# One head a step instead of two, and column loads two steps ahead, in a hybrid SSD and linear-attention layer

## The chip, the cores and the metric

The kernel runs on one core of a Trainium2 chip. The metric is the device time of one execution in microseconds, as a median over runs. The core has a matrix engine (TensorE, PE in the profile; its weight loads are shown apart as PEld), three engines for elementwise work (VectorE or DVE, ScalarE or ACT, GpSimd or POOL), and SyncE (SP), which in this kernel only issues transfers. Transfers are also issued from ScalarE's queue.

## The reference

One layer of a decoder runs over 16 meta tokens and 2048 real tokens of width 1024, in float32. A single input projection of the normed input feeds two branches: a Mamba-2 branch (SSD, 16 heads in 4 groups) and gated linear attention (GLA, 4 heads with key width 128 and value width 256). Each branch is projected, gated and merged, and the layer ends with an output projection and two RMS norms. Cut to what this change touches:

```python
u = rmsnorm(hres, norm_w)
proj = jnp.einsum('bld,dn->bln', u, w_in)
z, xbc, dt_raw, q, k, v, g_gla, a_lr, merge_g = split_cols(proj, IN_WIDTHS)
...
gate_logit = jnp.einsum('blr,rk->blk', a_lr, gla_gate_w2) + gla_gate_b
log_a = (jax.nn.log_sigmoid(gate_logit.astype(jnp.float32)) / GLA_GATE_TEMP)
log_a = log_a.reshape(b, l, GLA_HEADS, GLA_HEAD_K)
...
gc = jnp.cumsum(to_chunks(log_a).astype(jnp.float32), axis=3)
...
g_last = gi[:, :, -1]
k_dec = ki * jnp.exp(g_last[:, :, None, :] - gi)
s_new = jnp.exp(g_last)[..., None] * s + jnp.einsum('bhsk,bhsv->bhkv', k_dec, vi)
```

So the decay of a GLA head is a projection of rank 16 followed by a log-sigmoid and a cumulative sum along time; it is small beside the projections of `u`.

## The kernel before

**Two parts.** The first part, up to about 1500 us, does all that is sequential: the norm, the feature projections, the convolution, both scans. The second part does the merge gates, the two branch projections and the output projection as Strassen-like products of half-size blocks. Every product of the projections is made of three matmuls of values split into a high and a low float32r part (`accum`, L187 to L191).

**Blocks and steps.** The first part goes through four blocks of 512 tokens (block 0 also has the 16 meta tokens, and so processes its columns in two segments of 264). A block has eight units: four SSD groups (`ssd_proj`) and four GLA heads (`gla_proj`), of six steps each. All the work that isn't the projection itself is written as Python generators (the scans, the decays, the load of the next block, partial sums for the second part). After every step of a projection, `step()` advances each running generator to its next `yield`, so a `yield` decides between which projections an instruction stands.

**Order.** Within `manual_schedule`, TensorE and SyncE take their instructions in program order. The orders of VectorE, ScalarE and GpSimd are made by a planner that simulates the program when it is built; at run time each engine works strictly in its order.

**Banks and slots.** PSUM pool `pj` has three banks (`bufs=3`); a projection of block 0 takes two at once, of the later blocks one, and a token projection (`proj_tok`) of z or v holds two over its two steps. A bank or slot is taken again when all that read it are through. Weights lie in four slots (`whl`, `load_w`, L165), raw weights and operands of the partial sums in four (`wr`).

**The decays.** `gates(o)` begins with SSD group 1 of each block. Its first step transposes the low-rank activations. Then, for each pair of heads, one step makes both heads' projections (L485), empties each bank twice (L487 on VectorE, L488 on ScalarE) and applies Exp and Ln to the pair (L490, L491); two further steps do the subtraction and the cumulative sums (L494, L496). The first `gla_scan`, which reads the result, begins after the first GLA unit.

**The next block's columns.** `fetch_u(b + 1)` begins with the first GLA unit of a block. Its generator `load_u` first loads the next block's rows and makes the reciprocal norms (five steps). Then it loads the transposed input in eight columns of 128 x 512 (`fetch`, L308 to L311, into tag `acc`, four slots), and in each of eight steps issues the next column's load, scales the present one (L253, VectorE), copies its high part (L257, ScalarE), stores it to memory from ScalarE's queue (L259), and subtracts for the low part (L262, VectorE). The loads are issued by SP, whose queue also carries the weights (L169, L173), the saving of split weights (L185) and the loads and stores of partial sums (L76, L88). If a slot isn't free, SP waits at the load, and all behind it with it.

**Where the scans wait.** In `gla_scan`, four chunks follow each other: TensorE multiplies with the state (L880), VectorE updates the state (L883), and the next chunk's L880 needs it. L794 is a small VectorE copy in the scans of block 0 that a TensorE transpose (L796) needs.

Of the kernel before, what the change touches and what calls it, by code (L numbers as in the profile page):

```python
# [16 lines left out]
KT = 8  # L17
META = 16
BLK = 512
# [21 lines left out]
def trunk_kernel(ctx: ExitStack, tc: tile.TileContext, xm, xmt, w_feat, w_tok, w_zm, w_br, w_o,  # L41
# [7 lines left out]
    def mk(pool, shape, dt, tag, **kw):  # L49
        cnt[0] += 1  # L50
        return pool.tile(shape, dt, tag=tag, name=f"{tag}_{cnt[0]}", **kw)
# [83 lines left out]
    def bank(pool, tag):  # L135
        return mk(pool, [P, 512], F32, tag)
# [111 lines left out]
    def u_pair(tt):  # L248
        pair = mk(upool, [P, 2, KT * (META + BLK)], F32R, "u")[:, :, :KT * tt]
        return [pair[:, i].rearrange("p (k t) -> p k t", k=KT) for i in range(2)]  # L250

    def scale_u(kt, xk, rbc):
        nc.vector.scalar_tensor_tensor(xk, xk, norm_w[:, kt:kt + 1], rbc, op0=ALU.mult, op1=ALU.mult)  # L253

    def to_u(b, kt, xk, uh, ul):
        m0 = 0 if b else META
        nc.scalar.activation(uh[:, kt, :m0 + BLK], xk, AF.Copy)  # L257
        if b:
            nc.scalar.dma_start(u_left[b][kt], xk[:, m0:])  # L259
        else:  # L260
            u_stores.append((u_left[b][kt], xk[:, m0:]))
        nc.vector.tensor_tensor(ul[:, kt, :m0 + BLK], xk, uh[:, kt, :m0 + BLK].bitcast(F32), op=ALU.subtract)  # L262
# [41 lines left out]
    def load_u(b):  # L304
        row0 = META + b * BLK
        uh, ul = u_pair(BLK)

        def fetch(src):  # L308
            xt = mk(wk, [P, META + BLK], F32, "acc", bufs=4)[:, :BLK]
            nc.sync.dma_start(xt, src)  # L310
            return xt  # L311

        def fetch_rows(c):
            r0 = row0 + c * P
            return [fetch(xm[r0:r0 + P, i * BLK:(i + 1) * BLK]) for i in range(2)]

        def rows_rstd(xts, n):
            ss = mk(sm, [P, 1], F32, "ss")
            s2 = mk(sm, [P, 2], F32, "ss2")
            for i, xt in enumerate(xts):  # L320
                nc.scalar.activation(xt, xt, AF.Square, accum_out=s2[:, i:i + 1])
            nc.vector.tensor_tensor(ss, s2[:, 0:1], s2[:, 1:2], op=ALU.add)
            r = mk(sm, [P, 1], F32, "rs1")
            nc.vector.tensor_scalar(r[:n], ss[:n], 1.0 / D, EPS, op0=ALU.mult, op1=ALU.add)
            nc.gpsimd.tensor_tensor(r[:n], r[:n], mhalf[:n, 0:1], op=ALU.pow)
            return r

        rs = []
        rows = fetch_rows(0)
        yield  # L330
        for c in range(NCH):
            got, rows = rows, fetch_rows(c + 1) if c + 1 < NCH else None
            rs.append(rows_rstd(got, P))
            yield
        rb = bank(pt, "pt")
        for c in range(NCH):
            nc.tensor.matmul(rb[:, c * P:(c + 1) * P], rs[c].to_broadcast([P, P]), ident, start=True, stop=True)
        rbc = mk(wk, [P, 3 + META + BLK], F32, "cin")[:, :BLK]
        nc.scalar.activation(rbc, rb, AF.Copy)
        cols = [fetch(xmt[:, 0, row0:row0 + BLK])]  # L340
        yield
        for kt in range(KT):
            if kt + 1 < KT:
                cols.append(fetch(xmt[:, kt + 1, row0:row0 + BLK]))
            xk = cols[kt]
            scale_u(kt, xk, rbc)
            to_u(b, kt, xk, uh, ul)
            yield
        return uh, ul
# [3 lines left out]
    def fetch_u(b):  # L353
        next_u[b] = yield from load_u(b)
# [110 lines left out]
    def gates(o):  # L465
        m0, tt, chunks, g_all = o.m0, o.tt, o.chunks, o.g_all
        ast = mk(wk, [P, META + BLK], F32R, "act", bufs=NACT)[:48, :tt]
        for a, n in ([(0, META), (m0, BLK)] if m0 else [(0, BLK)]):
            ps = bank(pt, "pt")
            for i, (ca, cn) in enumerate(chunks):  # L470
                if a <= ca < a + n:
                    nc.tensor.transpose(ps[:48, ca - a:ca - a + cn], o.alr[:cn, i], ident[:cn, :cn])
            nc.scalar.activation(ast[:, a:a + n], ps[:48, :n], AF.Copy)
            nc.vector.tensor_tensor(ast[:32, a:a + n], ps[:32, :n], ast[:32, a:a + n].bitcast(F32),
                                    op=ALU.subtract)
            nc.scalar.activation(ast[:16, a:a + n], ps[:16, :n], AF.Copy)
        yield
        for h2 in range(0, GH, 2):
            gmt = mk(wk, [P, 2, META + BLK], F32, "tok4", bufs=NT4)
            for h in (h2, h2 + 1):  # L480
                gm = gmt[:, h % 2, :tt]
                gb = gate_b[:, h:h + 1]
                for i, (a, n) in enumerate(o.segs_all):
                    ps = bank(*((pt, "pt") if i else (pj, "pj")))
                    nc.tensor.matmul(ps[:, :n], w2[:, h * P:(h + 1) * P], ast[:, a:a + n],  # L485
                                     start=True, stop=True)
                    nc.vector.tensor_scalar(gm[:, a:a + n], ps[:, :n], gb, 0.0, op0=ALU.add, op1=ALU.min)  # L487
                    nc.scalar.activation(g_all[:, h, a:a + n], ps[:, :n], AF.Abs, bias=gb)  # L488
            ga = g_all[:, h2:h2 + 2, :tt]
            nc.scalar.activation(ga, ga, AF.Exp, scale=-1.0)  # L490
            nc.scalar.activation(ga, ga, AF.Ln, bias=1.0)  # L491
            yield
            for h in (h2, h2 + 1):
                nc.vector.tensor_tensor(gmt[:, h % 2, :tt], gmt[:, h % 2, :tt], g_all[:, h, :tt], op=ALU.subtract)  # L494
                for a, n in chunks:
                    nc.vector.tensor_tensor_scan(g_all[:, h, a:a + n], ones[:, :n], gmt[:, h % 2, a:a + n], 0.0,  # L496
                                                 op0=ALU.mult, op1=ALU.add)
                yield
# [424 lines left out]
    with tc.manual_schedule(engines={mybir.EngineType.PE, mybir.EngineType.SP}):  # L923
        for b in range(nblk):
            o = new_block(b, next_u[b])
            for i in range(SG + GH):
                if (b, i) in beside:
                    begin(beside_unit(beside[b, i]))
                if i == 1:
                    begin(gates(o))  # L930
                if i == SG and b + 1 < nblk:
                    begin(fetch_u(b + 1))
                for _ in ssd_proj(o, i) if i < SG else gla_proj(o, i - SG):
                    step()
            save(0)
        while running or begun:
            step()
# [326 lines left out]
```

## Time and profile before

| | |
|---|---|
| runs | 2295.11, 2302.26, 2309.61 us (median 2302.26) |
| profiled execution | 2299.73 us, of which the span from the first to the last instruction is 2297.9 us |
| TensorE busy | 2229.1 us (97%) |
| VectorE busy | 1604.1 us (70%) |
| ScalarE busy | 1119.9 us (49%) |
| GpSimd busy | 709.8 us (31%) |
| transfers | 507.49 MB, mean 221 GB/s |

All times within the run are in microseconds from the start of the span. Matmuls overlap in the pipeline and their ends are modelled, so a busy TensorE isn't one at its peak. The granted clock of TensorE (PEclk) is 1.00 at full speed. A wait is put down to the instruction that ended it; where VectorE is in the way, the cause can stand further ahead in VectorE's order. L numbers are lines of the kernel before.

### The profile page before, as it was taken

To read this page: it belongs to the slowest core of one execution; us is meant where nothing else is said; L and a number is where in the kernel's file an instruction comes from. 1 tells how busy PE (TensorE), PEld (TensorE's weight loads), DVE (VectorE), ACT (ScalarE), POOL (GpSimd) and SP (SyncE) were. 2 spreads that over 40 slices of the span, in tenths; PEclk is the share of its full clock that TensorE was granted. 3 is DMA by queue.
4 is the path that set the end of the run, shared out by engine and by line. 5 is a ranking of instruction groups with operands and counts; after the bars stand their busy time and mean duration, and the time that the engine had idled before them with its cause. 6 is when DMAs were issued, how large, how long until landed. Compare 5 with 4: busy or idle time off the path is not lost.

```text
span 2297.9 us, 36268 instructions
## 1 busy us (share of the span) xinstructions
PE 2229.1 (97%) x12599; PEld 1945.8 (85%) x12599; DVE 1604.1 (70%) x3108; ACT 1119.9 (49%) x2508; POOL 709.8 (31%) x709
## 2 busy tenths in 40 slices
PE   6899999999999999999999999989999999999998
PEld 6899888888889989888988898868788888787786
DVE  5787766687775677676579666664768845787876
ACT  5565555454444454444455434464544545554443
POOL 3344533122221122211122100135425463425341
PEclk9999999999999999999999999999999999999999
DMA  7766865667886676886667655466768956778653
GB/s 254 230 223 232 285 236 204 202 199 236 257 288 193 207 226 210 275 267 213 198 221 229 210 168 161 147 219 214 237 231 255 268 189 215 255 263 233 190 186 110
DMA packets 296200, 507.49 MB, mean 221 GB/s; under 512 B 27104, under 2 KB 143072, under 8 KB 296016
## 3 DMA queue, kind: packets, MB, share of 16 engines
q1 hardware_dynamic: 217232, 413.76, 55.8%
q10 hardware_dynamic: 74016, 82.50, 10.4%
q0 software_dynamic: 4768, 8.92, 2.4%
q8 instruction: 99, 1.62, 0.3%
q14 instruction: 85, 0.70, 0.1%
HBM read 357.87 MB, written 147.19 MB: 220 GB/s over the span
## 4 chain that ended last, share of the span: by engine, by line
PE 73%; DMA 9%; DVE 7%; issue 5%; ACT 3%; POOL 2%; SPq 1%; ACTq 0%; POOLq 0%; DVEq 0%
PE pj L189 13%; PE pj L191 13%; PE pj L190 12%; PE psa L189 5%; PE psa L190 5%; PE psa L191 5%; PE psb L190 2%; PE psb L191 2%; PE psb L189 2%; DMA br<-br_t 2%; PE pc L616 2%; PE pc L780 2%; DVE b L1001 1%; DMA br<-gate_t 1%; PE pc L617 1%
## 5 line engine op out<-in xcount | busy, mean ns | idle before, releaser
L189 PE MATMUL pj<-u,whl 128*128 128x512 f32 (+1 forms) x1184 | 446.7, 377 | 9.7 <-ACT acc L526 5.1
L191 PE MATMUL pj<-u,whl 128*128 128x512 f32 (+1 forms) x1184 | 430.9, 364 | 0.0
L190 PE MATMUL pj<-u,whl 128*128 128x512 f32 (+1 forms) x1184 | 430.0, 363 | 0.0
L189 PE MATMUL pj<-whl,u 128*128 128x256 f32 (+1 forms) x992 | 289.2, 292 | 2.4 <-ACT u L257 2.2
L191 PE MATMUL pj<-whl,u 128*128 128x256 f32 (+1 forms) x992 | 282.8, 285 | 0.2 <-DVE u L262 0.2
L190 PE MATMUL pj<-whl,u 128*128 128x256 f32 (+1 forms) x992 | 282.5, 285 | 0.0
L189 PE MATMUL psa<-b,a 128*128 128x512 f32 x640 | 253.8, 397 | 11.8 <-ACT sn L1041 11.5
L189 PEld LDWEIGHTS pj<-u,whl 128*128 128x128 f32 x1184 | 224.8, 190 | 47.5 <-ACT acc L526 5.9
L191 PEld LDWEIGHTS pj<-u,whl 128*128 128x128 f32 x1184 | 224.2, 189 | 35.8
L190 PE MATMUL psa<-b,a 128*128 128x512 f32 x640 | 251.9, 394 | 2.0 <-DVE b L1001 2.0
L190 PEld LDWEIGHTS pj<-u,whl 128*128 128x128 f32 x1184 | 224.9, 190 | 33.4
L191 PE MATMUL psa<-b,a 128*128 128x512 f32 x640 | 251.7, 393 | 0.0
L1025 DVE TENSOR_TENSOR a<-ar,a 128x512 fp32r<-128x512 f32 x160 | 156.3, 984 | 75.2 <-ACT a L1024 74.9
L80 POOL TENSOR_TENSOR wr<-wr 128x256 f32<-128x256 f32 x80 | 65.1, 813 | 429.9 <-DMA wr<-u 175.1
L177 POOL TENSOR_TENSOR whl<-wr,whl 128x512 fp32r<-128x512 f32 (+1 forms) x100 | 138.6, 1394 | 184.0 <-ACT whl L176 144.1
L189 PEld LDWEIGHTS pj<-whl,u 128*128 128x128 f32 x992 | 190.4, 192 | 3.7 <-ACT u L257 2.3
L191 PEld LDWEIGHTS pj<-whl,u 128*128 128x128 f32 x992 | 190.2, 192 | 0.8 <-DVE u L262 0.8
L190 PEld LDWEIGHTS pj<-whl,u 128*128 128x128 f32 x992 | 190.4, 192 | 0.4
L1001 DVE TENSOR_TENSOR b<-br,b 128x512 fp32r<-128x512 f32 x196 | 151.7, 796 | 44.0 <-ACT b L1000 43.5
L1000 ACT ACTIVATE b<-br 128x512 fp32r<-128x512 f32 x196 | 118.9, 626 | 103.9 <-DMA br<-br_t 35.8
L530 DVE SCALAR_TENSOR_TENSOR acc<-cin,hcw,acc 128x512 f32<-128x512 f32 (+1 forms) x192 | 160.2, 835 | 12.2 <-ACT acc L526 10.2
L189 PEld LDWEIGHTS psa<-b,a 128*128 128x128 f32 x640 | 122.0, 191 | 42.1 <-ACT sn L1041 16.2
(285 smaller groups left out, 4933.8 us busy)
## 6 DMA issues: line engine op xcount, KB each, us to landing
whl<-k_s SPq DMA_DIRECT2D x96, 512.0 KB, 4.4
whl<-k_g SPq DMA_DIRECT2D x96, 512.0 KB, 4.3
whl<-k_v SPq DMA_DIRECT2D x48, 512.0 KB, 3.7
whl<-k_z SPq DMA_DIRECT2D x36, 512.0 KB, 4.0
wr<-in_w_feat SPq DMA_DIRECT2D x64, 256.0 KB, 4.5
k_s<-whl SPq DMA_DIRECT2D x32, 512.0 KB, 3.6
cb<-cumd ACTq DMA_DIRECT2D x64, 256.0 KB, 5.8
k_g<-whl SPq DMA_DIRECT2D x32, 512.0 KB, 4.0
```

Of the source, the lines that this page charges most:

```text
L80: nc.gpsimd.tensor_tensor(o, x, y, op=ALU.subtract)
L177: nc.gpsimd.tensor_tensor(hl[:, 1], raw, hl[:, 0].bitcast(F32), op=ALU.subtract)
L189: nc.tensor.matmul(ps, sh, mh, start=first, stop=False, **kw)
L190: nc.tensor.matmul(ps, sh, ml, start=False, stop=False, **kw)
L191: nc.tensor.matmul(ps, sl, mh, start=False, stop=last, **kw)
L530: nc.vector.scalar_tensor_tensor(acc, cin[:, k:k + tt], hcw[:, ti, k:k + 1], acc, op0=ALU.mult, op1=ALU.add)
L616: nc.tensor.matmul(py[:, h * 64:(h + 1) * 64], dm[:, h], xdt[:, h], start=True, stop=True)
L617: nc.tensor.matmul(py[:, 256:512], cf[:, a:a + P], s_ssd[:, g], start=True, stop=True)
L780: nc.tensor.matmul(ps[:, r * P:(r + 1) * P], kq[:, 2 * r * P:(2 * r + 1) * P], kq[:, (2 * r + 1) * P:(2 * r + 2) * P], start=True, stop=True)
L1000: nc.scalar.activation(t[:, 0], raw, AF.Copy)
L1001: nc.vector.tensor_tensor(t[:, 1], raw, t[:, 0].bitcast(F32), op=ALU.subtract)
L1025: nc.vector.tensor_tensor(t[:, 1], src, t[:, 0].bitcast(F32), op=ALU.subtract)
```

## The change

In `load_u` two columns are loaded before the first scaling step instead of one, and each step issues the load of the column after next. In `gates` the generator yields between the two heads of a pair, so that each head's projection and evacuation has a step of its own; Exp and Ln are still applied once for the pair, in the step of the second head.

```diff
@@ -337,11 +337,11 @@
         rbc = mk(wk, [P, 3 + META + BLK], F32, "cin")[:, :BLK]
         nc.scalar.activation(rbc, rb, AF.Copy)
-        cols = [fetch(xmt[:, 0, row0:row0 + BLK])]
+        cols = [fetch(xmt[:, kt, row0:row0 + BLK]) for kt in range(2)]
         yield
         for kt in range(KT):
-            if kt + 1 < KT:
-                cols.append(fetch(xmt[:, kt + 1, row0:row0 + BLK]))
+            if kt + 2 < KT:
+                cols.append(fetch(xmt[:, kt + 2, row0:row0 + BLK]))
             xk = cols[kt]
             scale_u(kt, xk, rbc)
             to_u(b, kt, xk, uh, ul)
@@ -478,6 +478,8 @@
         for h2 in range(0, GH, 2):
             gmt = mk(wk, [P, 2, META + BLK], F32, "tok4", bufs=NT4)
             for h in (h2, h2 + 1):
+                if h > h2:
+                    yield
                 gm = gmt[:, h % 2, :tt]
                 gb = gate_b[:, h:h + 1]
                 for i, (a, n) in enumerate(o.segs_all):
```

## The prediction

> **What bounds the kernel now.** I read the page first, then the list of waits of TensorE, then the timelines of the five places where a line of this change stands behind a wait.
>
> ```profile
> span 2297.9 us, 36268 instructions
> PE 2229.1 (97%) x12599; PEld 1945.8 (85%) x12599; DVE 1604.1 (70%) x3108; ACT 1119.9 (49%) x2508; POOL 709.8 (31%) x709
> ```
>
> TensorE is busy for all but 2297.9 - 2229.1 = 68.8 us. The change alters no arithmetic, so it can only move those 68.8 us and the pace of TensorE around them. The waits of TensorE say who ends them (total, times, longest, in us):
>
> ```profile
> PE psa L189 <- ACT sn L1041: 11.5, 9, 3.1
> PE pc L880 <- DVE s_gla L883: 6.9, 9, 2.9
> PE pj L189 <- ACT acc L526: 5.1, 4, 2.0
> ...
> PE pj L189 <- ACT g_all L488: 3.5, 2, 2.5
> ...
> PE pt L796 <- DVE bt L794: 1.9, 1, 1.9
> ```
>
> The first row is the Strassen part, which the diff leaves alone. L488 is the evacuation in `gates`, so the fourth row belongs to the first edit. L883 and L794 stand on VectorE among the column scalings of `load_u`, so these may belong to the second. The timeline of TensorE places the waits (start, duration, line, and in brackets the idle time and what ended it):
>
> ```profile
> 86.51 0.59 PE L189 MATMUL pj<-u,whl 128*128 128x264 f32 x1 [2.46 <-ACT g_all L488]
> 95.66 0.39 PE L189 MATMUL pj<-u,whl 128*128 128x264 f32 x1 [0.87 <-ACT acc L526]
> 115.08 0.39 PE L189 MATMUL pj<-u,whl 128*128 128x264 f32 x1 [1.07 <-ACT g_all L488]
> 280.46 0.28 PE L796 MATMUL pt<-cst,bt 128*32 128x128 f32 x1 [1.86 <-DVE bt L794]
> 688.25 0.70 PE L880 MATMUL pc<-s_gla,act 128*128 128x256 f32 x2 [1.92 <-DVE s_gla L883]
> 1045.67 1.22 PE L880 MATMUL pc<-s_gla,act 128*128 128x256 f32 x2 [2.94 <-DVE s_gla L883]
> ```
>
> Both gate waits lie in block 0; blocks 1 to 3 have none. A stall can cost more than its idle time. The table by stretches has the granted clock in the third column from the right:
>
> ```profile
> core 0: us, PE busy (x) PEld busy (x) DVE busy (x) ACT busy (x) POOL busy (x), PEclk, DMA share, GB/s
> 84.00:87.00 3.00, 0.54 (x3) 0.49 (x3) 3.00 (x11) 1.93 (x5) 0.00 (x0) 0.86 0.98 325
> 87.00:90.00 3.00, 3.00 (x17) 3.00 (x17) 2.31 (x9) 2.85 (x5) 0.00 (x0) 0.57 0.82 252
> ...
> 147.60:151.00 3.40, 3.40 (x18) 3.40 (x17) 3.37 (x6) 2.05 (x5) 1.74 (x2) 0.50 0.88 316
> 280.80:284.10 3.30, 3.30 (x18) 3.30 (x17) 2.82 (x8) 1.88 (x7) 0.46 (x1) 0.50 1.05 415
> 686.10:689.50 3.40, 1.48 (x8) 1.10 (x8) 3.37 (x9) 3.40 (x12) 0.00 (x0) 1.00 0.46 168
> 1045.40:1048.70 3.30, 3.02 (x7) 2.46 (x8) 1.90 (x4) 2.32 (x9) 0.00 (x0) 0.50 0.04 15
> ```
>
> After the wait of 2.46 us the clock lacks 3 x 0.14 + 3 x 0.43 = 1.71 us of full-speed time. So a stall that is followed by a half-clock stretch costs its idle time and 1.7 us more; those at 86, 280 and 1045 us are, the one at 688 us (clock 1.00) is not.
>
> **The change, first edit: one head a step.** Nothing is added or removed. In each block heads 1, 2 and 3 move one to two steps later, with their matmul (two in block 0), the L487 and L488 that empty each bank, and the Exp, Ln, subtractions and scans behind them; no DMA is among them. `gates` now takes nine steps instead of seven and is done some fifteen steps before the first `gla_scan` reads `g_all`, so the delay itself costs nothing.
>
> What ends the wait at 86.51 is a PSUM bank. `pj` has three. In block 0 the z projection has just used two, head 0 took the third, head 1 the first again, and a feature projection needs two at once (two segments); its second segment met the bank of head 0, which L488 had not emptied. With one head a step that projection can take the two z banks and head 0 keeps the third for a whole projection. The term: 2.46 + 1.07 for the two waits, 1.71 for the clock. What is late next: the projection after head 1 needs both banks of its forerunner, where otherwise one of them was longer free. That kind of wait stands at 95.66 (0.87), and I add it once; between none and once for each of the three places where a head now parts two projections is the bound (0 to 2.6 us). First edit: -2.46 - 1.07 - 1.71 + 0.87 = -4.4 us.
>
> The one new neighbourhood is head 3. It now falls between the two halves of group 2's z projection and takes the third bank while z holds two. The projection behind it then has to take the z bank just emptied by L516. In block 1 these rows, of the VectorE and the TensorE timeline, say what margin it has:
>
> ```profile
> 520.85 1.28 DVE L516 SCALAR_TENSOR_TENSOR tok<-tok,pj 128x512 f32<-128x512 f32 x2 [2.04 <-ACT tok L515]
> ```
>
> ```profile
> 522.13 0.48 PE L189 MATMUL pj<-u,whl 128*128 128x512 f32 x1
> ```
>
> The first of the two L516 is over at 520.85 + 1.28/2 = 521.5, the projection starts at 522.13: 0.6 us of cover. I cost it at nothing; if the cover goes, it is the slower rival below.
>
> **Second edit: columns two steps ahead.** Each of blocks 1 to 3 still issues eight column transfers on SP, in the same order; columns 1 to 7 move one step up, past the weight loads and, in some steps, the partial-sum loads and stores (L76, L88) of that step. POOL's queue issues none of this. What it can remove is VectorE's wait for the landing, which is 17.0 us in 14 places:
>
> ```profile
> DVE acc L253 <- DMA acc<-in_xmt: 17.0, 14, 2.5
> ```
>
> Most of that is off the path. Where it is on it, the rows of VectorE are these:
>
> ```profile
> 280.24 0.17 DVE L794 COPY bt<-act 128x32 f32<-128x32 f32 x1
> ...
> 682.72 0.75 DVE L253 SCALAR_TENSOR_TENSOR acc<-acc,pv,cin 128x512 f32<-128x512 f32 x1 [2.42 <-DMA acc<-in_xmt]
> 687.72 0.48 DVE L883 SCALAR_TENSOR_TENSOR s_gla<-s_gla,egl,pc 128x256 f32<-128x256 f32 x1
> ...
> 1039.62 1.26 DVE L253 SCALAR_TENSOR_TENSOR acc<-acc,pv,cin 128x512 f32<-128x512 f32 x1 [1.51 <-DMA acc<-in_xmt]
> 1045.14 0.48 DVE L883 SCALAR_TENSOR_TENSOR s_gla<-s_gla,egl,pc 128x256 f32<-128x256 f32 x1
> ```
>
> The last column of blocks 2 and 3 holds VectorE 2.42 and 1.51 us, and the L883 behind it, in an order that is fixed, is what TensorE waits for. Landing a step earlier, the column removes 1.92 us (all of the wait at 688, since 2.42 is more) and 1.51 of the 2.94 us at 1045. Whether the half-clock stretch at 1045 goes with it is open: 1.4 us of idle time remain, so I take half, 0.85, with 0 and 1.7 as ends. L794 at 280.24 has no column wait ahead of it that the rows show; I leave its 1.86 us. Second edit: -1.92 - 1.51 - 0.85 = -4.3 us.
>
> What it adds: `acc` has four slots, and column k+2 takes the slot of column k-2, two steps old where it was three. SP waits for that slot until the forerunner's store to memory (L259) has landed, and everything behind it on SP waits too.
>
> ```profile
> 262.95 0.78 SPq L310 DMA_DIRECT2D acc<-in_xmt  x1
> ...
> 275.32 0.33 SPq L185 DMA_DIRECT2D k_v<-whl  x1
> ...
> 646.66 0.73 SPq L310 DMA_DIRECT2D acc<-in_xmt  x1
> 648.97 3.05 SPq L169 DMA_DIRECT2D whl<-k_v  x2
> ...
> 1002.85 0.97 SPq L310 DMA_DIRECT2D acc<-in_xmt  x1
> 1005.15 3.04 SPq L169 DMA_DIRECT2D whl<-k_v  x2
> ```
>
> ```profile
> 268.37 0.33 ACTq L259 DMA_DIRECT2D u<-acc  x1
> ...
> 644.00 0.33 ACTq L259 DMA_DIRECT2D u<-acc  x1
> ...
> 1000.57 0.33 ACTq L259 DMA_DIRECT2D u<-acc  x1
> ```
>
> ```profile
> whl<-k_v SPq DMA_DIRECT2D x36, 512.0 KB, 4.0
> ...
> u<-acc ACTq DMA_DIRECT2D x24, 256.0 KB, 4.7
> ```
>
> The places 262.95, 646.66 and 1002.85 are where column 4 would now be issued; the store of column 0 starts at 268.37, 644.00 and 1000.57 and takes 4.7 us. So SP would stand until about 273.1, 648.7 and 1005.3: 10, 2.0 and 2.4 us. In block 1 SP's next long pause ends only at 275.32, so the stand mostly replaces that one. In blocks 2 and 3 the next weight load went out at 648.97 and 1005.15 anyway. TensorE uses a tile in about 2.7 us (the two loads from 648.97 span 3.05 us; one issue of 0.33 off), has three of the four tiles in hand when a load is issued, and the load lands in 4.0 us: 3 x 2.7 - 4.0 = 4.1 us of slack. I cost the new wait at nothing.
>
> **The sum.** -4.4 - 4.3 = -8.7 us. The profiled execution took 2299.73 us (1.8 more than its span), which gives 2291.0. The median of the three runs, 2302.26, is 2.5 above that execution, and the same saving from it gives 2293.6; since a median is asked for I say **2294**.
>
> A rule speaks for less. The Trainium skill, "TensorE: Matmul & The Clock Gate", "Why this matters for your kernels", warns only of idle gaps of more than about 3 us between matmuls; none of these five is that long, and by it the clock terms, 1.71 + 0.85, would be nothing. The row 87.00:90.00 at 0.57 behind a 2.46 us gap, and 147.60:151.00 at 0.50, do not agree with that rule, and the measurement decides. Part 1 of that page lets a free-running window of 3413 ns set the clock, and with that the phase counts too.
>
> **Rivals.** (a) *The stalls go, the half clock falls elsewhere.* The 1.92 us stall at 688 left the clock at 1.00, the 1.86 us stall at 280 halved it: position decides, and a shift of some us moves all later positions. Then 1.71 + 0.85 come back: 2296. It is also what the page's rule would give.
>
> (b) *Everything near these lines goes*: 2.46 + 1.07 + 1.86 + 1.92 + 2.94 = 10.25 of idle time and three half-clock stretches, 5.1: 2302.3 - 15.4 = 2287. For it: the planner gets earlier columns and can order VectorE anew. Against: L794 and the rest of the 2.94 us have other work ahead of them.
>
> (c) *The waits change their name.* VectorE's and ScalarE's orders come from a planner, and with SP standing for a slot a column lands little sooner; new waits of the size of the L526 and L883 rows replace the old: 2302. For it: those two rows together are 12 us in small pieces.
>
> (d) *Slower: the bank of head 3.* If L516 (or L515 ahead of it) is more than 0.6 us later in group 2, which now also has head 2's subtraction and scans in that step, TensorE waits as it did at 86.51. At that price, 2.46 + 1.71 in each of four blocks, it costs 16.7, less the 8.7 saved: +8.0, 2310. Against it: L516 comes earlier in the program than the scans, and the planner goes by that.
>
> **How the numbers follow.** Forecast 0.50 (its own range, by the bounds of its terms, 2289 to 2300), a 0.13, b 0.10, c 0.17, d 0.10. About 1% is what a measurement of this kernel can tell from no change, 23 us. All five cases lie within it. Faster than 2279 would take (b) and 8 us from waits the diff does not touch: 0.04. Slower than 2325 would take (d) with SP's slot stands turned into weight waits beyond the 4.1 us of slack: 0.04. Within: 0.92. The range, 2282 to 2309, takes in b and c with the 7 us by which the runs differ, and most of d.
>
> **What would show it.** Right: no L189 <- L488 wait near 86 and 115 us; no half-clock stretch at 86; L253's waits for in_xmt well under 17.0 us; no L880 wait above 1.5 us near 688 and 1045. Wrong: TensorE waiting at a group 2 projection for L516 or L515 (d); SP's L310 waiting for a store of `acc` followed by TensorE waiting for a weight DMA; L880 waits as before though L253 no longer waits, which would mean that VectorE's order and not the landing made L883 late.

## The result, and the profile after

The changed kernel is slower: 2320.05 us in the median of six runs (2315.18 to 2324.66), against 2299.41 us for the kernel before, measured beside it (2294.66 to 2309.61). The ratio is 1.0078, with a 95% interval of 1.0059 to 1.0098, so some 18 us were lost. That is less than 1%, but clearly no gain. 2294 had been forecast, and the range ended at 2309. Its profiled execution took 2321.71 us, 22.0 more than that of the kernel before.

From the line behind the added `yield` on, lines stand two further down than before: L488 is now L490, L491 is L493, L494 is L496, L496 is L498, L516 is L518, L526 is L528, L578 is L580, L607 is L609, L616 is L618, L883 is L885. In an experiment the shift can be larger; each is told with its own rows.

First the page's totals, then TensorE's waits (total, times, longest, in us), both of the kernel after.

```profile
span 2319.9 us, 36266 instructions
PE 2235.1 (96%) x12599; PEld 1946.4 (84%) x12599; DVE 1607.1 (69%) x3108; ACT 1121.0 (48%) x2508; POOL 706.7 (30%) x709
```

```profile
PE psa L189 <- ACT sn L1043: 19.0, 11, 3.1
...
PE pc L618 <- DVE sq L609: 11.1, 3, 3.9
PE pj L189 <- ACT acc L528: 7.0, 5, 2.5
...
PE pc L882 <- DVE s_gla L885: 1.7, 6, 0.5
...
PE pj L189 <- DVE tok L518: 0.9, 1, 0.9
```

Of what was forecast, this is here: the two waits for the evacuation of a decay (L490, 3.5 us before) are gone, and the GLA scan's wait for VectorE (L885) fell from 6.9 to 1.7 us. What was not forecast is the second row. Three waits, up to 3.9 us each, end with L609, a multiplication of the SSD scan that the diff doesn't touch; before, TensorE's list of waits had none for L607. TensorE's timeline places them:

```profile
510.64 0.50 PE L487 MATMUL pj<-act,w 48*128 48x512 f32 x1
...
528.39 1.97 PE L618 MATMUL pc<-c,sq 128*128 128x64 f32 x8 [3.40 <-DVE sq L609]
...
892.18 1.05 PE L618 MATMUL pc<-c,sq 128*128 128x64 f32 x7 [3.90 <-DVE sq L609]
...
1253.47 1.10 PE L618 MATMUL pc<-c,sq 128*128 128x64 f32 x8 [3.81 <-DVE sq L609]
```

They come once in each of blocks 1, 2 and 3, in SSD group 2, each some 18 us behind head 3's projection (510.64 in block 1). The table by stretches, of the kernel after and then of the kernel before for the first place, has the granted clock in the third column from the right:

```profile
527.80:534.50 6.70, 6.11 (x18) 5.21 (x19) 6.70 (x16) 2.40 (x5) 2.38 (x4) 0.50 0.48 161
893.00:896.30 3.30, 3.30 (x10) 2.70 (x10) 3.30 (x6) 0.36 (x2) 1.53 (x2) 0.50 0.51 151
1254.80:1258.10 3.30, 3.30 (x10) 2.53 (x9) 3.30 (x8) 0.00 (x0) 0.85 (x2) 0.50 0.34 100
```

```profile
527.80:534.50 6.70, 6.70 (x37) 5.78 (x36) 5.36 (x11) 2.43 (x5) 3.63 (x6) 1.00 1.02 298
```

Behind each wait TensorE runs at half clock for 3.3 to 6.7 us, where before it had the full clock (1.00 at the other two places, too). That loses half of 13.3 us, 6.7 us, and with the idle time of 11.1 us makes 17.8 us, about the size of the loss. Whether it is the loss, the experiments have to show.

The balance of the two profiled executions points the same way. Cut where the second part's products begin (at 1504.5 before, 1517.8 after), the table by stretches gives:

```profile
0.00:1504.50 1504.50, 1457.22 (x9240) 1311.16 (x9240) 1043.29 (x2361) 730.74 (x1796) 381.90 (x445) 0.99 0.69 221
```

```profile
0.00:1517.80 1517.80, 1462.05 (x9240) 1311.53 (x9240) 1048.61 (x2361) 731.32 (x1796) 381.35 (x445) 0.99 0.68 219
```

The same 9240 matmuls keep TensorE busy 4.8 us longer, and it is idle for 55.8 instead of 47.3 us: 13.3 us net in the first part, after the savings and what came back of them. The other 8.7 us lie in the second part, which the change does not touch; how far one pair of profiles bears this out is told at the end of the experiments.

### The profile page after: what moved, and what is told of

Same layout as the page of the kernel before. It is cut to its first block, busy times and chain, and to the rows that moved or that the text cites. A ratio compares the mean times of both kernels' runs of the same rounds, so it can differ in the third digit from the quotient of the medians.

```text
span 2319.9 us, 36266 instructions
## 1 busy us (share of the span) xinstructions
PE 2235.1 (96%) x12599; PEld 1946.4 (84%) x12599; DVE 1607.1 (69%) x3108; ACT 1121.0 (48%) x2508; POOL 706.7 (30%) x709
## 4 chain that ended last, share of the span: by engine, by line
PE 54%; DMA 5%; DVE 5%; issue 3%; ACT 3%; SPq 1%; POOL 0%; ACTq 0%; DVEq 0%; POOLq 0%
PE pj L189 8%; PE pj L191 8%; PE pj L190 8%; PE psa L189 5%; PE psa L191 5%; PE psa L190 5%; PE psb L191 2%; PE psb L189 2%; PE psb L190 2%; DMA br<-br_t 2%; PE pc L782 1%; PE psc L191 1%; PE psc L190 1%; PE psc L189 1%; DVE b L1003 1%
## 5 line engine op out<-in xcount | busy, mean ns | idle before, releaser
L189 PE MATMUL pj<-u,whl 128*128 128x512 f32 (+1 forms) x1184 | 446.4, 377 | 9.3 <-ACT acc L528 7.0
L190 PE MATMUL pj<-u,whl 128*128 128x512 f32 (+1 forms) x1184 | 429.7, 363 | 0.0
L189 PE MATMUL pj<-whl,u 128*128 128x256 f32 (+1 forms) x992 | 288.7, 291 | 2.4 <-ACT u L257 2.2
L190 PE MATMUL pj<-whl,u 128*128 128x256 f32 (+1 forms) x992 | 282.0, 284 | 0.0
L189 PE MATMUL psa<-b,a 128*128 128x512 f32 x640 | 254.0, 397 | 19.3 <-ACT sn L1043 19.0
L189 PEld LDWEIGHTS pj<-u,whl 128*128 128x128 f32 x1184 | 224.5, 190 | 46.4 <-ACT acc L528 8.3
L190 PE MATMUL psa<-b,a 128*128 128x512 f32 x640 | 252.2, 394 | 2.0 <-DVE b L1003 2.0
L190 PEld LDWEIGHTS pj<-u,whl 128*128 128x128 f32 x1184 | 224.4, 189 | 33.5
L189 PEld LDWEIGHTS pj<-whl,u 128*128 128x128 f32 x992 | 189.9, 191 | 5.3 <-ACT u L257 2.4
L190 PEld LDWEIGHTS pj<-whl,u 128*128 128x128 f32 x992 | 189.9, 191 | 0.3
L532 DVE SCALAR_TENSOR_TENSOR acc<-cin,hcw,acc 128x512 f32<-128x512 f32 (+1 forms) x192 | 157.4, 820 | 13.3 <-ACT acc L528 12.2
L189 PEld LDWEIGHTS psa<-b,a 128*128 128x128 f32 x640 | 121.9, 191 | 50.3 <-ACT sn L1043 24.4
```

The costliest lines, as they stand in the source:

```text
L189: nc.tensor.matmul(ps, sh, mh, start=first, stop=False, **kw)
L190: nc.tensor.matmul(ps, sh, ml, start=False, stop=False, **kw)
L532: nc.vector.scalar_tensor_tensor(acc, cin[:, k:k + tt], hcw[:, ti, k:k + 1], acc, op0=ALU.mult, op1=ALU.add)
```

## The experiments

**Which edit.** Each edit alone. As in the prediction, the first edit is one head a step (the diff's second hunk), and the second is the columns:

```diff
# gates_only: the change with the hunk of the columns undone
-        cols = [fetch(xmt[:, kt, row0:row0 + BLK]) for kt in range(2)]
+        cols = [fetch(xmt[:, 0, row0:row0 + BLK])]
...
-            if kt + 2 < KT:
+            if kt + 1 < KT:
# columns_only: the change with the hunk of the heads undone
-                if h > h2:
-                    yield
```

> Only the first edit: one head a step, columns as before. Theory (heads 2 and 3 now meet the start of the SSD scan of group 1): nearly the whole loss is here. In the trace of after, TensorE falls back by 7.7, 5.6 and 6.6 us at group 2 of blocks 1, 2 and 3 (3.4 to 3.9 us of waiting for L609 each, plus half-clock stretches) and gains 2 us in block 0, so the first part is about 18 us longer than before; the whole 2315 to 2325 us, ratio 1.006 to 1.010. Rival (the second edit's loads bring the loss): the ratio is below 1.002 and the L618 waits are gone.

> Only the second edit: columns two steps ahead, gates as before. Theory: it is worth a gain of 0 to 5 us in the first part (the L880 waits of 1.92 and 2.94 us near 688 and 1045 us are gone, as in after), so 2294 to 2302 us, ratio 0.997 to 1.001. Rival (the loads or SP's stands for a slot are the loss): 2310 us or more, ratio above 1.004.

Measured: one head a step alone 1.0089 (1.0074 to 1.0104), the columns alone 0.9989 (0.9975 to 1.0003). The loss belongs to the first edit, whole. TensorE's waits in the kernel with the first edit alone:

```profile
PE pc L618 <- DVE sq L609: 10.7, 3, 3.9
PE pc L882 <- DVE s_gla L885: 6.7, 9, 3.2
```

The L609 waits are there without the columns, and the L885 waits stay at 6.7 us, so it was the columns that took those away.

The kernel before, unchanged, shows what a repetition gives:

> The kernel before, unchanged, for a second trace. The second part is 8.6 us longer in the trace of after (from 1502 us on), though every engine's order there is the same. If that is the scatter of transfers between executions, the second part of this trace differs by several us from the first trace of before, and the ratio is 1.000 within 0.002. If it belongs to the change, the second part is within 2 us of the first trace.

Measured: 0.9997 (0.9983 to 1.0012).

**Which heads.** Here heads 0 and 1 get steps of their own, and their sums share one step, so that heads 2 and 3 stay where they were.

```diff
@@ gates, in the kernel before
             for h in (h2, h2 + 1):
+                if h == 1:
+                    yield
...
-                yield
+                if h:
+                    yield
```

> Heads 0 and 1 in steps of their own, their two scans then in one step, so that heads 2 and 3 stay together and where they were. Theory: block 0 keeps its gain of 2 to 4 us (no wait for L488 at 86 us), group 2 of blocks 1 to 3 has no wait for L609; 2294 to 2300 us, ratio 0.997 to 1.001. Rival (any splitting of a pair costs, by its banks): ratio 1.004 or more.

Measured: 1.0002 (0.9987 to 1.0017). To split the first pair costs nothing and brings nothing. The loss needs the second pair at its new place.

**What of the second pair: its sums or its Exp and Ln?** The kernel before, with no split, but the second pair's sums (in the other kernel, its Exp, Ln and sums) written two steps later:

```diff
# scans_late
             nc.scalar.activation(ga, ga, AF.Ln, bias=1.0)
             yield
+            if h2:
+                yield
+                yield
# exp_late
+            if h2:
+                yield
+                yield
             ga = g_all[:, h2:h2 + 2, :tt]
             nc.scalar.activation(ga, ga, AF.Exp, scale=-1.0)
```

> The kernel before, with nothing changed but that the subtraction and cumulative sums of heads 2 and 3 stand two steps later (where after has them); heads 2 and 3 and their Exp and Ln stay where they were. In after, the wait for L609 in group 2 of blocks 1 to 3 is 3.4 to 3.9 us; 2.7 us of these sums lie on VectorE between the z evacuation and L609, and Exp, Ln and two table loads hold the z evacuation on ScalarE back by about 2.5 us. Theory A (the sums on VectorE make the wait): each of the three waits is 3 us or more, the loss is that of after, ratio 1.005 to 1.010. Theory B (Exp, Ln and the table loads make it): the waits are under 1 us, ratio under 1.002. Both in part: waits of 1 to 2.5 us.

> Heads 2 and 3 projected together where they were in before, but their Exp and Ln two steps later (between the halves of group 2's z projection) and the sums behind these, as in after: the split of the pair alone is taken out. Theory (what is moved under the start of the scan makes the loss, not the splitting or the PSUM banks): waits for L609 of 3 to 4 us and the whole loss, ratio 1.006 to 1.010. Rival (head 3's bank between the z halves): ratio under 1.002.

Measured: 1.0003 (0.9989 to 1.0017) and 1.0007 (0.9994 to 1.002). These are not the answers they were meant to be, because the edits moved nothing. The orders of VectorE (3108 instructions), ScalarE (2483) and GpSimd (709) are the same as in the kernel before, position by position. ScalarE's timeline, of the kernel before and of the one with Exp and Ln written two steps later:

```profile
505.74 1.06 ACT L490 ACTIVATE g_all<-g_all 128x1024 f32<-128x1024 f32 x1
...
507.89 1.28 ACT L491 ACT_TABLE_LOAD   x1
509.19 1.06 ACT L491 ACTIVATE g_all<-g_all 128x1024 f32<-128x1024 f32 x1
```

```profile
502.25 1.06 ACT L493 ACTIVATE g_all<-g_all 128x1024 f32<-128x1024 f32 x1
...
504.32 1.28 ACT L494 ACT_TABLE_LOAD   x1
505.61 1.06 ACT L494 ACTIVATE g_all<-g_all 128x1024 f32<-128x1024 f32 x1
```

Exp and Ln stand where they stood (that execution was some 3.5 us ahead as a whole). In this kernel a `yield` fixes the order of TensorE and SyncE alone; the other engines' order is the planner's, and here it put the work back where its data, the projections, let it stand. So it looks as if the first edit moved the Exp, Ln and sums of heads 2 and 3 by moving their projections; `pair_in_z` below tries that.

The same two yields on top of the first edit:

```diff
# split_scans_later: gates_only, and
             nc.scalar.activation(ga, ga, AF.Ln, bias=1.0)
             yield
+            if h2:
+                yield
+                yield
```

> One head a step as in the first edit, but the sums of heads 2 and 3 two steps later still, so that they come after the start of the SSD scan; Exp and Ln stay between the z halves. Theory A (sums on VectorE): the waits for L609 are under 1 us, ratio 0.998 to 1.002. Theory B (Exp, Ln and table loads): waits of 2.5 us or more remain, ratio above 1.004.

Measured: 1.0099 (1.0064 to 1.0134), with the waits as before, now at `PE pc L621 <- DVE sq L612: 13.2, 3, 5.0`. To write the sums later cures nothing. This time the yields do move something, 28 positions of VectorE's order and 20 of ScalarE's against the first edit alone, so the program's order isn't quite without effect; but in block 1 all the sums still stand ahead of the scan's multiplication.

**Keep the split, move the place earlier.** One head a step, but a pair's sums in one step, which brings head 2 forward by one step and head 3, and with it Exp and Ln, too:

```diff
# split_tight: gates_only, and
-                yield
+                if h:
+                    yield
```

> One head a step, but the sums of heads 0 and 1 (and of heads 2 and 3) in one step each instead of two, so that head 2 is one step and head 3, Exp and Ln one step earlier than in after, ahead of group 2's z projection, and all the sums of heads 2 and 3 one step ahead of the scan's start. Theory A or B: no wait for L609 above 1 us; block 0 keeps its gain of 2 to 4 us; 2294 to 2302 us, ratio 0.997 to 1.001. Rival (one head a step costs by itself): ratio above 1.004.

Measured: 1.003 (1.0015 to 1.0044), and no L609 wait. About two thirds of the loss are gone. The ratio lies between the two that were expected (up to 1.001, or above 1.004): something is left that isn't the L609 wait. TensorE's list has a new name, a normalisation on ScalarE (L650 there, 2.6 us in three places), but the columns alone, which lose nothing, have 1.6 us of the same wait. What the rest is stays open.

**Take links out of the chain.** The first edit, once with the logarithm of heads 2 and 3 replaced by a copy (so that ScalarE has no ACT_TABLE_LOAD for it; those decays aren't computed), once with the cumulative sums of heads 2 and 3 left out:

```diff
# no_ln: gates_only, and
-            nc.scalar.activation(ga, ga, AF.Ln, bias=1.0)
+            if h2:
+                nc.scalar.activation(ga, ga, AF.Copy)
+            else:
+                nc.scalar.activation(ga, ga, AF.Ln, bias=1.0)
# no_sums: gates_only, and
-                for a, n in chunks:
+                for a, n in chunks if h2 == 0 else []:
```

> The first edit alone (one head a step), with the Ln of heads 2 and 3 replaced by a plain copy, which leaves out their logarithm and with it the table loads (1.28 us each, one before Ln, one before the tanh of z). With the first edit alone the waits for L609 in group 2 of blocks 1 to 3 are 3.4, 3.5 and 3.9 us. If ScalarE is the head of the chain (Exp, table, Ln, table, then the tanh of z and the sums), each wait shrinks by the 2.6 us left out, to about 1 us, and the ratio comes to 1.002 or less. If only VectorE's sums count, the waits stay at 3 us or more and the ratio above 1.005.

> The first edit alone, with the cumulative sums of heads 2 and 3 left out (eight instructions of 0.34 us a block; the subtraction before them stays). If VectorE's sums count, each wait for L609 shrinks by their 2.7 us, to 1 us or less, ratio 1.002 or less. If only ScalarE counts, the waits stay at 3 us or more.

Measured: 1.0021 (1.0001 to 1.0042) and 1.0012 (0.9998 to 1.0025). The waits of TensorE for L609 (L612 in the first kernel) were 10.7 us and are now, in the kernel without the logarithm and in the one without the sums:

```profile
PE pc L621 <- DVE sq L612: 2.9, 3, 1.1
```

```profile
PE pc L618 <- DVE sq L609: 1.2, 3, 0.4
```

Taking out either link is enough to end most of the wait: two table loads (2 x 1.28 us) are 2.6 us per block, the sums 2.7 us, and without the one or the other a wait of about 3.6 us is 2.6 or 3.2 us shorter. The first of the two kernels is the cleaner one: it has 17 table loads instead of 25, and all 3108 positions of VectorE's order are those of the first edit alone. Without the sums the planner also ordered their neighbours anew (64 positions of ScalarE's order differ). So the wait is the sum of a chain over two engines, which the rows of the kernel after show in block 1. ScalarE first, then VectorE:

```profile
513.54 0.67 ACT L490 ACTIVATE g_all<-pj,pv 128x512 f32<-128x512 f32 x1
514.23 0.60 ACT L517 ACTIVATE tok<-pj 128x512 f32<-128x512 f32 x1
514.73 1.05 ACT L492 ACTIVATE g_all<-g_all 128x1024 f32<-128x1024 f32 x1
515.80 1.28 ACT L493 ACT_TABLE_LOAD   x1
517.09 1.06 ACT L493 ACTIVATE g_all<-g_all 128x1024 f32<-128x1024 f32 x1
518.17 1.28 ACT L517 ACT_TABLE_LOAD   x1
519.46 0.60 ACT L517 ACTIVATE tok<-pj 128x512 f32<-128x512 f32 x1
```

```profile
514.86 0.69 DVE L518 SCALAR_TENSOR_TENSOR tok<-tok,pj 128x512 f32<-128x512 f32 x1 [2.94 <-ACT tok L517]
518.18 1.29 DVE L496 TENSOR_TENSOR tok<-tok,g_all 128x512 f32<-128x512 f32 x2 [2.63 <-ACT g_all L493]
520.09 0.69 DVE L518 SCALAR_TENSOR_TENSOR tok<-tok,pj 128x512 f32<-128x512 f32 x1 [0.62 <-ACT tok L517]
520.70 2.00 DVE L498 TENSOR_TENSOR_SCAN g_all<-ones_r,tok 128x128 f32<-128x128 f32 x6
522.61 0.67 DVE L580 TENSOR_TENSOR sq<-pc,cst 128x512 f32<-128x512 f32 x1
...
524.97 0.73 DVE L498 TENSOR_TENSOR_SCAN g_all<-ones_r,tok 128x128 f32<-128x128 f32 x2
525.61 2.12 DVE L606 TENSOR_SCALAR sq<-cb,ntc 128x128 f32<-128x128 f32 x8
527.65 0.68 DVE L609 TENSOR_TENSOR sq<-sq,sq 128x512 f32<-128x512 f32 x1
```

The z projection of group 2 has two halves. ScalarE takes the tanh of the first (L517 at 514.23), then Exp and Ln of the decays with a table load on either side of the Ln, and the second tanh comes only at 519.46. VectorE, in the planner's order, has the subtraction of the decays (L496) between the two L518, which empty z's banks. So it stands idle for 2.63 us until the Ln is through, subtracts for 1.29 us, and waits another 0.62 us for the second tanh: the second L518 comes 5.23 us behind the first (514.86 to 520.09). Without the logarithm it comes 3.25 us behind (510.86 to 514.11 there). The sums of the decays follow, 2.00 and 0.73 us, ahead of and amid the SSD scan's L580, L606 and L609; and TensorE, whose next instruction needs L609, stands from 525.0 to 528.39. Before, Exp and Ln were through at 510.25, the eight sums were done by 515.5 us, and the scan's multiplication came at 526.04, early enough for TensorE's L616 at 528.05 to start without a wait. VectorE's timeline, before:

```profile
512.16 1.05 DVE L496 TENSOR_TENSOR_SCAN g_all<-ones_r,tok 128x128 f32<-128x128 f32 x3
...
513.77 1.68 DVE L496 TENSOR_TENSOR_SCAN g_all<-ones_r,tok 128x128 f32<-128x128 f32 x5
...
526.04 1.28 DVE L607 TENSOR_TENSOR sq<-sq,sq 128x512 f32<-128x512 f32 x2
```

On the two table loads: the Trainium skill, "ScalarE: Activation LUTs", "What ACT_TABLE_LOAD costs", gives 1283 ns a load, which these rows show, and some 1380 ns of drain beside it, which they don't: load and activation follow each other within 0.03 us.

**The place without the split.** In the kernel before, both heads of the second pair are projected in one step again, but that step comes two steps later, between the two halves of z. So that no third bank is needed there, head 3 takes its bank from another pool:

```diff
# pair_in_z, against the kernel before
+            if h2:
+                yield
+                yield
             gmt = mk(wk, [P, 2, META + BLK], F32, "tok4", bufs=NT4)
...
-                    ps = bank(*((pt, "pt") if i else (pj, "pj")))
+                    ps = bank(*((pt, "pt") if i or h == 3 else (pj, "pj")))
```

> No head is split from its pair, but heads 2 and 3 are projected together two steps later than in before, between the halves of group 2's z projection, where the first edit has head 3 (head 3 takes its bank from the other PSUM pool, since the z projection holds two of three). Moving the Exp, Ln or sums by yields alone changed no order on ScalarE or VectorE, so it is the place of the projection on TensorE that moves them. If so, this has the whole loss: waits for L609 of 3 to 5 us, ratio 1.005 to 1.010. If it is the splitting, or head 3's bank in the pool of the z projection, no such waits, ratio under 1.002.

Measured: 1.0066 (1.0049 to 1.0084). Its waits of TensorE, and its timeline of ScalarE:

```profile
PE pc L619 <- DVE sq L610: 11.6, 3, 4.0
```

```profile
512.30 1.05 ACT L493 ACTIVATE g_all<-g_all 128x1024 f32<-128x1024 f32 x1
513.37 1.28 ACT L494 ACT_TABLE_LOAD   x1
...
515.74 1.28 ACT L518 ACT_TABLE_LOAD   x1
517.04 0.60 ACT L518 ACTIVATE tok<-pj 128x512 f32<-128x512 f32 x1
```

The same waits and most of the loss, with nothing split. The place between the halves of z makes these waits, and neither the split nor the third bank of `pj` is needed for them. The ratio is below the 1.0089 of the first edit, though the two intervals overlap, so a smaller part of the loss may still belong to the split.

**And past the place.** The first edit with the second pair two steps later still, behind the z projection:

```diff
# split_late: gates_only, and
+            if h2:
+                yield
+                yield
             gmt = mk(wk, [P, 2, META + BLK], F32, "tok4", bufs=NT4)
```

> One head a step, but heads 2 and 3 two steps later than in the first edit: head 2 behind group 2's z projection, head 3 behind the next projection, so that Exp, Ln and sums fall behind the start of the scan. If the place counts: no L609 wait above 1 us at the start of group 2, ratio 0.998 to 1.002; a new wait a few us later in the scan is possible, and would be a wait for L609 or L625 of its later chunks. If one head a step costs wherever it stands: ratio above 1.005.

Measured: 1.0029 (1.0008 to 1.0051), again with no wait for the scan's multiplication. On either side of the z halves these waits are gone. But here, too, the ratio lies between the two that were expected: both kernels are still 0.3% slower than the kernel before, with intervals clear of none.

That gives the price of the waits from runs, beside that from rows. Against the first edit alone (1.0089), the two kernels with the second pair elsewhere and the two with a link left out are 0.6 to 0.8% lower, some 14 to 18 us (each taken against the kernel before on its own chip). So the waits, with the half clock behind them, are most of the loss; the remaining 0.1 to 0.3% stays open.

**Is the first edit's gain in block 0 there?** The second edit, with the split in block 0 only, beside the second edit alone:

```diff
# columns_block0: the change, but
-                if h > h2:
+                if h > h2 and m0:
                     yield
# columns_alone_5: the change without these two lines
```

> The second edit, and the first edit in block 0 alone, where its two waits for L488 stood. If the loss is all at group 2 of blocks 1 to 3, this keeps what both edits gain: 2 to 4 us from the banks of block 0 and 1 to 5 us from the columns, ratio 0.996 to 0.999. If one head a step costs as much in block 0 as it saves (its places there have new waits for L528 in the traces so far), the ratio is that of the columns alone.

> The second edit alone once more, with more rounds: 0.9989 within 0.9975 to 1.0003 left open whether it gains. If the two L880 waits of 1.9 and 2.9 us at the end of the columns are its worth, the ratio is 0.998 to 0.999 and below 1 with its interval. If SP's stands for a slot give it back, 1.000.

Measured: 1.0001 (0.9988 to 1.0013) with the split in block 0, 0.9983 (0.9971 to 0.9995) without it. So the split brings nothing in block 0 either, and may cost some 4 us (0.18%; the two intervals overlap). The timeline of TensorE with the split shows what took the place of the two waits:

```profile
101.61 0.39 PE L189 MATMUL pj<-u,whl 128*128 128x264 f32 x1 [2.47 <-ACT acc L528]
...
142.97 0.39 PE L189 MATMUL pj<-u,whl 128*128 128x264 f32 x1 [0.86 <-DVE tok L518]
...
153.86 0.39 PE L189 MATMUL pj<-u,whl 128*128 128x264 f32 x1 [2.27 <-ACT acc L528]
```

The L528 waits, 5.1 us before, are 7.7 us in this kernel, and 0.86 us for L518 is new: together 3.5 us, as much as the two waits that went. The size is that of one profile: in four executions with the orders of the kernel before (below) the waits of this name vary from 4.1 to 6.4 us. But the stalls of 2.47 us near 102 us and of 0.9 us near 143 us stand in all three kernels that split the pairs of block 0 as the change does. Of the clock, the stretches from 87 and from 147.6 us on are at 1.00 here (0.57 and 0.50 before), but the 5 us from 153 on at 0.67 (1.00 before).

The columns alone are the fastest kernel here, though by little: 2299.62 against 2303.78 us for the kernel before on the same chip, a gain of 0.17%, with the interval clear of none in this run, though not in the shorter one above (0.9975 to 1.0003). TensorE's row for the GLA scan there is `PE pc L880 <- DVE s_gla L883: 2.0, 7, 0.5`, where it was 6.9 us.

**How much one profile says.** Four executions have one and the same order of VectorE, ScalarE and GpSimd: the kernel before, its repetition, and the two kernels whose yields moved nothing. TensorE's timeline in each, in that order, and in the kernel after last, at the first L190 wait of the Strassen products, where the second part begins:

```profile
1504.59 0.79 PE L190 MATMUL psa<-b,a 128*128 128x512 f32 x1 [2.03 <-DVE b L1001]
```

```profile
1499.01 0.79 PE L190 MATMUL psa<-b,a 128*128 128x512 f32 x1 [2.02 <-DVE b L1001]
```

```profile
1500.79 0.80 PE L190 MATMUL psa<-b,a 128*128 128x512 f32 x1 [2.02 <-DVE b L1004]
```

```profile
1500.29 0.79 PE L190 MATMUL psa<-b,a 128*128 128x512 f32 x1 [2.03 <-DVE b L1004]
```

```profile
1517.88 0.79 PE L190 MATMUL psa<-b,a 128*128 128x512 f32 x1 [2.02 <-DVE b L1003]
```

With spans of 2297.9, 2294.4, 2301.2 and 2299.9 us, what follows this point takes 793.3, 795.4, 800.4 and 799.6 us, and 802.0 us in the kernel after (2319.9 - 1517.88). So with nothing changed the first part differs by 5.6 us and the second by 7.1, and the profile of the kernel before happened to have the longest first part and the shortest second. Against the means of the four, 1501.2 and 797.2, the kernel after has 16.7 us more in the first part and 4.8 in the second. The first is far outside the scatter; whether the second is chance, one profile can't tell, and it stays open. Most of it has one name: TensorE's wait `psa L189 <- ACT sn` of the Strassen products takes 19.0 us in the kernel after and 11.5 in the kernel before, but 15.3, 18.1 and 14.8 us in the other three.

## Why the prediction was wrong

The step that failed is the sentence that `gates` "is done some fifteen steps before the first `gla_scan` reads `g_all`, so the delay itself costs nothing". A deadline far ahead says that nothing waits for the moved work. It doesn't say what waits behind it. I asked when its result is read, and not which instructions it now stands among on ScalarE and VectorE. (Nor was the deadline so far ahead: by ScalarE's timeline in the kernel after, L733, the first instruction of a `gla_scan`, reads the decays in the same group at 522.10, after 0.88 us of waiting for the first sums.) It moved from 505–515 us, where those engines had slack, into the one stretch of the group where tanh, the emptying of z and the scan's multiplications follow one another on the way to TensorE. By the rows quoted, 4.7 us of Exp, Ln and table loads (514.73 to 519.46) stand ahead of the second tanh, and 1.29 us of subtractions and 2.73 us of sums stand ahead of L609; of all this TensorE felt 3.4 to 3.9 us, once in each of blocks 1 to 3. Costed at nothing, this term measured 17.8 us by the rows, and some 14 to 18 us by the runs without these waits.

**Rival (d)** had the place (group 2, head 3 between the halves of z, each block) and nearly the price (16.7 us before savings), but the wrong object. It was the bank that L516 empties; in blocks 1 to 3 no projection waits for it in the kernel after. VectorE's rows from 518.18 on show that its thought was half right: the second L518 was late, behind the subtraction and for want of the tanh; but what TensorE missed first was L609. What I set against (d), that "the planner goes by that", the order of the program, didn't hold as a rule: two kernels with work written two steps later kept every position, and a third moved only 28 of 3108 on VectorE.

**First edit, -4.4 us.** The two waits went as forecast, 3.5 us and the half clock behind the one at 86 us with them. What is late next was sized at 0.87 us, with 2.6 as the bound; in the kernel with the split in block 0 only it is 3.5 us (2.6 more for L528 and 0.9 for L518), beyond the bound, and the 2.47 us stall at 101.61 alone is larger than the whole term that I took. Measured, the term is not -4.4 but lies between about nothing (the first pair alone, 1.0002) and +4 us.

**Second edit, -4.3 us.** Right in its steps and about right in its size: alone it measured 0.9989 and 0.9983, that is -2.5 and -3.9 us, the latter between -6.7 and -1.2. VectorE's wait for the landing of a column, in the kernel after:

```profile
DVE acc L253 <- DMA acc<-in_xmt: 9.4, 6, 2.7
```

It was 17.0 us in 14 places. No L882 wait is longer than 0.5 us, so the stalls at 688 and 1045 are gone, the second wholly and not by the 1.51 that I took. The term for the clock, 0.85, rested on one execution, and so did the nothing at 688 us. Of the four executions with the same orders, two had half clock behind the stall near 1045 us (2.94 and 2.01 us long) and two hadn't (1.45 and 1.63 us); near 688 us two had (2.52 and 1.97 us) and two hadn't (1.92 and 1.91 us). One wait grew: that for L794 (now L796), 1.9 us before, is 2.5 us in all four kernels with the columns. The new wait of SP's queue stood as predicted, and cost nothing:

```profile
SPq L310 <- DMA u<-acc: 10.5, 3, 7.4
```

Three stands in all, the longest in block 1, where 10 us had been expected; TensorE's list shows no wait for a weight.

**The chances.** Within 1% had 0.92, and 1.0078 is within 1%. The number and the range missed: the range stopped at (d) as a net of +8, and no case had the price of a new stall in three blocks together with an edit that saves nothing in block 0. Nor is 1% the least that can be told from no change, as I wrote: the interval of the result reaches 0.2% to either side.

## What to carry to other kernels

When work is moved, its deadline is the lesser question. List, for each engine that it uses, what stands there at the new place and who waits for that; two table loads and eight short sums, free at one place, cost some 14 to 18 us a run two steps on. Before moving work by the program's order, find out which engines follow the program: here a planner ordered the others, later `yield`s moved little or nothing, and the place of the instruction that made the data ready (a matmul of 0.5 us) moved all that followed it. And a change of two parts is worth taking apart, as one of them may be a gain: the columns alone measured 0.9983 and 0.9989 of the kernel before.

## What the runs showed of the hardware

Stalls of 3.40, 3.90 and 3.81 us were followed by half clock for 6.7, 3.3 and 3.3 us, so the clock added from 0.4 of the idle time to nearly the whole of it, and the most behind the shortest stall. With the first edit alone, the stall at the first place was 3.40 us again and the half clock behind it 3.4 us. So the length of a stall doesn't settle what follows. At 280 us a stall of 1.86 us brought half clock in the kernel before, while stalls of 1.87, 1.87 and 1.86 us in the other three executions with its orders brought none.

The clock records in the trace of the kernel before show what else counts. Up to 1400 us, stretches of half clock start at 86.16, 147.60, 280.72, 434.32 and 1045.31 us. Each lasts 3.41 us, and they start 18, 39, 45 and 179 times 3.413 us apart. They stand on one grid in time, so where a stall falls on that grid counts beside its length, as rival (a) had it. A term for the clock taken from one execution is therefore a matter of luck.

And the scatter of either part, 5.6 and 7.1 us in four executions whose engines all kept the same order, is larger than what either edit was forecast to bring.
